# A two-layer hybrid decoder trunk on one core: where block products' weights begin in SBUF, and norms by transposes

## The chip, the cores and the metric

The kernel runs on one core of one Trainium2 chip. The metric is the device time of one execution in microseconds. All numbers are float32 in memory; most matmuls read them as float32r after a split into a first part (rounded) and a second part (what the rounding left).

## The reference

Two layers over 512 tokens of width 1024. Layer 0 mixes by sliding-window attention and a short gated convolution, layer 1 by chunked gated linear attention; behind each mixer follow a gated MLP with a causal convolution of width 3 and a gated per-layer embedding. Every part begins with an RMS norm.

```python
def _rms_norm(x, gain):
    xf = x.astype(jnp.float32)
    y = xf * lax.rsqrt(jnp.mean(xf * xf, axis=-1, keepdims=True) + RMS_EPS)
    return (y * gain.astype(jnp.float32)).astype(x.dtype)

def _conv_ffn(h, w_up, conv_w, conv_b, w_down):
    u = _causal_depthwise_conv(h @ w_up, conv_w) + conv_b
    gate, up = jnp.split(u, 2, axis=-1)
    return (jax.nn.gelu(gate, approximate=False) * up) @ w_down

def _per_layer_embedding(x, p_i, norm, w_gate, w_proj):
    gate = jax.nn.sigmoid(_rms_norm(x, norm) @ w_gate)
    return gate * (p_i @ w_proj)

def reference(x, p, ...):
    for i in range(DEPTH):
        h = _rms_norm(x, mix_norm[i])
        x = x + (_attn_conv_mixer if i % 2 == 0 else _gla_mixer)(h, ...)
        x = x + _conv_ffn(_rms_norm(x, ffn_norm[i]), ...)
        x = x + _per_layer_embedding(x, p[i], ...)
    return x
```

## The kernel before

The activations lie transposed in SBUF (`xT`, eight tiles of 128 features by 512 tokens). A weight matrix is loaded in blocks by DMAs of SyncE's queue (`raw`), and each block is split in two: ScalarE copies it into the first part `wh`, VectorE subtracts that and writes the second part `wl` (`cut`, L118 to L152). A product of the two splits takes three matmuls (`mm3`, L153): first by first, first by second, second by first.

There are two kinds of product. *Full* products (`mm3`, L157 to L159) have a stationary operand of 128 by 128 weights and stream 512 tokens. *Block products* (`seven`, L835 on, matmuls on L850 to L852) form two column blocks of the MLP's matrices by a scheme of seven products of half blocks instead of eight; each has four steps of three matmuls, and each matmul streams 256 tokens against 128 by 128 weights. Their weights are made by `first_forms`, `more_forms` and `cut_blocks` (L789 on): blocks of the matrix and differences of blocks, split into `wh` and `wl` tiles of 1024 columns or, where smaller, into tiles of 512 columns (`t2`, in the buffers of tag `sq`).

In the up-projection of each MLP (`ffn`) a loop runs over eleven groups: in each, two columns of the second half of the matrix by full products and two of the first by seven block products. The order of TensorE's instructions is written out by hand there (`manual_schedule`), and so it is in the down-projection (`down`), where a `plan` lists full and block units, and in the last stage (`ple1`), where the orders of VectorE and ScalarE are written out too. Elsewhere a planner orders the work of each engine. Each engine works its queue in order.

A norm is in three pieces. While the features of a stage come out, ScalarE squares them and VectorE adds the squares up in `acc` (128 features by 512 tokens). `end_norm` (L316) sums over features: four matmuls with `acc` as the stationary operand and one column of ones as the moving one give the sums, tokens on partitions; `rsqrt` (L161) scales them on VectorE and raises them to the power -1/2 on GpSimd, which gives `r`. Products run on unnormed activations meanwhile; their results are multiplied by the factor later. Where tokens lie along the free axis, the factor is needed on all partitions: `spread` (L329) splits `r` in two, builds two diagonal tiles `dg` on VectorE, multiplies each by a square of ones on TensorE, and ScalarE copies the result to `R`. `end_norm` takes the sums so in five norms; `spread` is called five times.

A column of vectors (biases, taps, gains) is turned by `columns` (L198), which writes it into a tile that is kept. The taps of the two MLPs have tiles of their own, `vfa0` and `vfb0`, `vfa1` and `vfb1`.

Of the kernel before, what the change touches and what calls it, by code (L numbers as in the profile page):

```python
# [14 lines left out]
ALU = mybir.AluOpType  # L15
# [41 lines left out]
class Kernel:  # L57
# [35 lines left out]
    def four(self, pool, dtype=F32R):  # L93
        return pool.tile([P, 4, S], dtype, tag="four", name=self.nm("four"), bufs=7)

    def split(self, hl, src, gain=None):

        nc = self.nc
        h, l = hl
        if gain is None:  # L100
            nc.scalar.activation(h, src, AF.Copy)
            nc.vector.tensor_tensor(l, src, h.bitcast(F32), ALU.subtract)
        else:
            nc.scalar.activation(h, src, AF.Copy, scale=gain)
# [10 lines left out]
        t = self.wp.tile([P, 2048], F32, tag="raw", name=self.nm("raw"), bufs=2)  # L115
        return t[:, : na * nb].rearrange("p (a b) -> p a b", b=nb)

    def cut(self, rv, by, pool=None, bufs=3):  # L118


        nc = self.nc
        pool = pool or self.wp
        na, nb = rv.shape[1:]
        parts = []
        n = 2 if na * nb > 1024 else 1
        for k in range(n):
            if by == "b":
                a, b = na, nb // n
                v = rv[:, :, k * b : (k + 1) * b]
            else:  # L130
                a, b = na // n, nb
                v = rv[:, k * a : (k + 1) * a, :]
            h = pool.tile([P, 1024], F32R, tag="wh", name=self.nm("wh"), bufs=bufs)
            l = pool.tile([P, 1024], F32R, tag="wl", name=self.nm("wl"), bufs=bufs)
            hv = h[:, : a * b].rearrange("p (a b) -> p a b", b=b)
            lv = l[:, : a * b].rearrange("p (a b) -> p a b", b=b)
            nc.scalar.activation(hv, v, AF.Copy)  # L137
            nc.vector.tensor_tensor(lv, v, hv.bitcast(F32), ALU.subtract)  # L138
            parts.append((hv, lv))

        def get(i, c0, c1):
            if by == "b":
                b = nb // n
                k = c0 // b
                h, l = parts[k]
                return h[:, i, c0 - k * b : c1 - k * b], l[:, i, c0 - k * b : c1 - k * b]
# [23 lines left out]
    def setup(self):  # L170
        nc, a = self.nc, self.a
        self.mhalf = self.cp.tile([P, 32], F32, name="mhalf")[:, :16]
        self.cf = self.cp.tile([P, P + 64 + 256], F32, name="cf")
        self.ident = self.cf[:, :P]
        self.ones = self.cp.tile([P, P], F32, name="ones")
        self.ones_r = self.cp.tile([P, P], F32R, name="ones_r")
        self.nowhere = self.pa()
        with self.tc.manual_schedule(engines={ET.PE, ET.DVE, ET.Activation}):
            nc.vector.memset(self.ones, 1.0)
            nc.vector.tensor_copy(self.ones_r, self.ones)  # L180
            nc.vector.memset(self.mhalf, -0.5)
            nc.scalar.dma_start(self.ident, a["cst_f"][:, :P])
            self.vec0 = self.load_vectors0()
            self.idle(7)
        self.invf = self.cf[:, P + 32 : P + 64]
        self.amask = self.cf[:, P + 64 :]

# [10 lines left out]
    def columns(self, name, views, q=None):  # L198

        nc = self.nc  # L200
        n = sum(v.shape[0] for v in views)
        rows = self.sp.tile([P, P], F32, tag="vrow", name=self.nm("vrow"))
        if q is None and self.gate is not None:
            self.late(rows[:, :1])
        at = 0
        for v in views:
            (q or nc.gpsimd).dma_start(rows[at : at + v.shape[0], :], v)
            at += v.shape[0]
        if q:

            nc.scalar.copy(self.few(4, "rs", 4), self.mhalf[:, :4])
        col = self.cp.tile([P, -(-n // 64) * 64], F32, name=name)[:, :n]
# [31 lines left out]
    def load_vectors_ffn(self, i):  # L244
        a = self.a
        w = a["ffn_conv_w"][i].rearrange("j (c p) -> j c p", p=P)
        b = a["ffn_conv_b"][i].rearrange("(c p) -> c p", p=P)
        va = self.columns(f"vfa{i}", [w[0], w[1]])
        vb = self.columns(f"vfb{i}", [w[2], b])
        self.fcv = [va[:, :44], va[:, 44:], vb[:, :44], vb[:, 44:]]  # L250


# [5 lines left out]
    def advance(self, m, gain, src=None):  # L258
# [6 lines left out]
        if m == 0:  # L265
            nc.scalar.activation(self.acc, x, AF.Square)
        else:
            sq = self.sp.tile([P, S], F32, tag="sq", name=self.nm("sq"), bufs=2)
            nc.scalar.activation(sq, x, AF.Square)
            nc.vector.tensor_tensor(self.acc, self.acc, sq, ALU.add)  # L270

    def squares(self, m):
# [1 line left out]
        if m == 0:  # L274
            nc.scalar.activation(self.acc, x, AF.Square)
        else:
            sq = self.sp.tile([P, S], F32, tag="sq", name=self.nm("sq"), bufs=2)
# [38 lines left out]
    def end_norm(self, sums=None):  # L316

        nc = self.nc
        if sums is None:
            ps = self.pa()  # L320
            for t in range(NT):
                nc.tensor.matmul(
                    ps[:, t : t + 1], self.acc[:, t * P : (t + 1) * P], self.ones[:, :1], start=True, stop=True
                )
            sums = ps[:, :NT]
        self.r = self.few(NT, "rtok")
        self.rsqrt(self.r, sums, 1.0 / D)

    def spread(self):  # L329

        nc = self.nc
        rh = self.sm.tile([P, 8], F32R, tag="rhi", name=self.nm("rhi"))[:, :NT]
        rl = self.few(NT, "rlo")
        nc.scalar.activation(rh, self.r, AF.Copy)
        nc.vector.tensor_tensor(rl, self.r, rh.bitcast(F32), ALU.subtract)
        pr = self.pa()
        for i, x in enumerate((rh.bitcast(F32), rl)):
            dg = self.sp.tile([P, NT, P], F32R, tag="sq", name=self.nm("dg"), bufs=2)
            nc.vector.tensor_tensor(
                dg, self.ident.unsqueeze(1).to_broadcast([P, NT, P]),  # L340
                x.unsqueeze(2).to_broadcast([P, NT, P]), ALU.mult,
            )
            nc.tensor.matmul(pr, self.ones_r, dg.rearrange("p a b -> p (a b)"), start=i == 0, stop=i == 1)
        R = self.sp.tile([P, S], F32, tag="R", name=self.nm("R"))
        nc.scalar.copy(R, pr)
        return R
# [77 lines left out]
    def mixer0(self):  # L424
        nc, a, tc = self.nc, self.a, self.tc
        with tc.tile_pool(name="m0", bufs=1) as mp:
# [65 lines left out]
            sink = self.sm.tile([P, 16], F32, name="sink", bufs=1)[:, :NQ]  # L492
# [182 lines left out]
            def conv_taps(j2):  # L675
                for c in range(2):
                    j = 2 * j2 + c
                    xs = mp.tile([P, S], F32, tag="cxs", name=self.nm("cxs"), bufs=2)
                    pad = mp.tile([P, S + 64], F32, tag="pad", name=self.nm("pad"), bufs=2)[:, : S + 2]
                    nc.scalar.copy(xs, pss["x", c])  # L680
                    nc.gpsimd.memset(pad[:, :2], 0.0)
                    nc.vector.tensor_tensor(pad[:, 2:], pss["c", c], R2, ALU.mult)
# [106 lines left out]
    def cut_blocks(self, src, wide=True):  # L789

        nc = self.nc
        if wide:
            h, l = (self.wp.tile([P, 1024], F32R, tag=g, name=self.nm(g), bufs=3) for g in ("wh", "wl"))
        else:
            h, l = (self.sp.tile([P, S], F32R, tag="sq", name=self.nm("t2"), bufs=2) for _ in range(2))
        h, l = (x.rearrange("p (j n) -> p j n", n=src.shape[2]) for x in (h, l))
        nc.scalar.activation(h, src, AF.Copy)  # L797
        nc.vector.tensor_tensor(l, src, h.bitcast(F32), ALU.subtract)  # L798
# [10 lines left out]
    def first_forms(self, ev, od, raw=None):  # L809
# [3 lines left out]
        if raw is not None:  # L813
            plain = self.cut_blocks(raw[:, :, :P])
        else:
            h, l = (self.wp.tile([P, 1024], F32R, tag=g, name=self.nm(g), bufs=3) for g in ("wh", "wl"))
            h, l = (x.rearrange("p (j u n) -> p j u n", u=2, n=P) for x in (h, l))
            for u, b in enumerate((b11, b21)):
                self.split((h[:, :, u], l[:, :, u]), b)
# [61 lines left out]
    def ffn(self, i, project, next_gain):  # L881
# [8 lines left out]
        with tc.tile_pool(name=f"ffn{i}", bufs=1) as fp:  # L890
# [5 lines left out]
                return fp.tile([P, 2, S], F32, tag="zt", name=self.nm("zt"), bufs=2)  # L896

            def taps(y, ps, f, more=None):
                z = fp.tile([P, S + 2], F32, tag="z", name=self.nm("z"), bufs=3)[:, :S]
                if more is None:  # L900
                    nc.vector.tensor_tensor(z, ps, R, ALU.mult)
                else:
# [398 lines left out]
    def ple1(self, fp):  # L1301
# [16 lines left out]

        def chunk(src):
            if count[0] % 6 < 3:  # L1320
                h, l = (self.wp.tile([P, 2, H], F32R, tag=g, name=self.nm(g), bufs=3) for g in ("wh", "wl"))
            else:
                four = self.four(fp)
                h, l = four[:, :2], four[:, 2:]
# [45 lines left out]
            return pj  # L1370

        def result():
            return fp.tile([P, S + 2], F32, tag="z", name=self.nm("so"), bufs=3)[:, :S]

        def keep(banks, tag):
            out = []
# [33 lines left out]
        with tc.manual_schedule(engines={ET.PE, ET.DVE, ET.Activation}):  # L1410
# [4 lines left out]
            add(None, "s1", wt1, first=True, order=steps[:2])  # L1415

            self.end_norm()
            ka = [self.sp.tile([P, S], F32, tag=g, name=self.nm("keep"), bufs=n) for g, n in (("acc", 1), ("sq", 2))]
            for k, x in zip(ka, X):
                nc.scalar.copy(k, x)  # L1420
            wt2 = chunks(b11)
# [10 lines left out]
            kb = [self.sp.tile([P, S], F32, tag="sq", name=self.nm("keep"), bufs=2), result()]  # L1432
# [45 lines left out]
    def mixer1(self):  # L1478
# [4 lines left out]
        with tc.tile_pool(name="m1", bufs=1) as mp:  # L1483
# [285 lines left out]
            def read(h):  # L1769
# [12 lines left out]
                        mm(po, Ec[:, c], st[:, j - 1, :], start=False, stop=True)  # L1782
                    pos.append(po)
                for j, po in enumerate(pos):
                    sq = self.sp.tile([P, GDV], F32, tag="sq", name=self.nm("osq"), bufs=2)
# [161 lines left out]
```

## Time and profile before

| | |
|---|---|
| median of 3 runs | 1223.96 us (1223.2 to 1224.04) |
| profiled execution, first to last instruction | 1221.9 us |
| granted TensorE clock, mean | 0.999 |
| TensorE busy | 1215.3 us, 7040 matmuls |
| VectorE busy | 972.8 us |
| ScalarE busy | 667.0 us |
| HBM | 95 GB/s over the span |

The profile page shows the busy time of each engine over the span (PE is TensorE's matmuls, PEld its weight loads, DVE VectorE, ACT ScalarE, POOL GpSimd), the span in 40 slices with the busy share in tenths, the chain of work that ended last, and the costliest groups of instructions with the names of their tiles (`pa` and `ps` are PSUM, `a`, `b` and `four` split activations). In the lists in order of time a row has the start in us, the duration in us, the engine, the line, the operation, output and inputs, and the shape. The end of a matmul is modelled, and matmuls overlap, so the time that one costs is the step from its start to the next one's start. In a table of stretches each engine has its busy time and, in brackets, the number of instructions; behind them stand the granted clock, the DMA share and GB/s.

### The profile page before, as it was taken

How to read it: one execution, taken by the hardware profiler on the slowest of the kernel's cores; microseconds unless marked ns; L12 is line 12 of the kernel's file. 1: busy time of each engine (PE TensorE's matmuls, PEld its weight loads, DVE VectorE, ACT ScalarE, POOL GpSimd, SP SyncE). 2: the span in 40 equal slices, each digit the busy share in tenths (PEclk: the TensorE clock that was granted, in tenths of full speed). 3: DMA queues.
4: the chain of work that ended last, by engine and by line, in shares of the span. 5: the costliest groups of instructions: out<-in, count | busy, mean ns of one | idle time of the engine just before them, and what ended most of it. 6: DMA issues, size and time to landing. Idle time of an engine off the chain costs nothing.

```text
span 1221.9 us, 17764 instructions
## 1 busy us (share of the span) xinstructions
PE 1215.3 (99%) x7040; PEld 1055.2 (86%) x7040; DVE 972.8 (80%) x1539; ACT 667.0 (55%) x1087; POOL 43.5 (4%) x64
## 2 busy tenths in 40 slices
PE   9999999999999999999999999999999999999998
PEld 8877789999899889888988988889999999888887
DVE  6886587899998996746679876678999888978595
ACT  7466455656555644534573555555565545645374
POOL 2500000000000000000100000000000000000000
PEclk9999999999999999999999999999999999999999
DMA  7221322423233242222322222322242423322601
GB/s 218 78 97 40 100 72 69 138 70 117 91 103 105 87 138 96 95 74 98 122 92 68 71 70 69 104 75 99 71 137 69 139 69 120 131 86 95 207 1 69
DMA packets 111271, 117.61 MB, mean 96 GB/s; under 512 B 2856, under 2 KB 106466, under 8 KB 111188
## 3 DMA queue, kind: packets, MB, share of 16 engines
q1 hardware_dynamic: 109824, 115.35, 28.9%
q8 instruction: 55, 0.90, 0.3%
q0 software_dynamic: 560, 0.42, 0.3%
q10 hardware_dynamic: 804, 0.70, 0.2%
q14 instruction: 28, 0.23, 0.1%
HBM read 114.37 MB, written 2.10 MB: 95 GB/s over the span
## 4 chain that ended last, share of the span: by engine, by line
PE 88%; DVE 8%; ACT 2%; issue 2%; POOL 1%; DVEq 0%; ACTq 0%; POOLq 0%
PE ps L157 12%; PE ps L158 12%; PE ps L159 12%; PE pa L158 7%; PE pa L157 7%; PE pa L159 7%; PE ps L850 6%; PE ps L852 6%; PE ps L851 6%; PE pa L852 2%; PE pa L851 2%; PE pa L850 2%; DVE wl L138 1%; PE ps L1347 1%; PE ps L1349 1%
## 5 line engine op out<-in xcount | busy, mean ns | idle before, releaser
L137 ACT ACTIVATE wh<-raw 128x1024 fp32r<-128x1024 f32 (+4 forms) x154 | 152.4, 992 | 150.7 <-PE ps L158 107.3
L138 DVE TENSOR_TENSOR wl<-raw,wh 128x1024 fp32r<-128x1024 f32 (+4 forms) x154 | 175.2, 1139 | 49.9 <-ACT wh L137 49.2
L797 ACT ACTIVATE wh<-raw 128x1024 fp32r<-128x1024 f32 x78 | 82.7, 1060 | 127.5 <-DVE raw L822 63.7
L910 DVE SCALAR_TENSOR_TENSOR zt<-z,vfa,zt 128x510 f32<-128x510 f32 (+1 forms) x176 | 130.8, 745 | 11.9 <-ACT zt L908 11.2
L798 DVE TENSOR_TENSOR wl<-raw,wh 128x1024 fp32r<-128x1024 f32 x78 | 95.4, 1223 | 20.3 <-ACT wh L797 20.1
L908 ACT ACTIVATE zt<-z,vfb 128x512 f32<-128x512 f32 x88 | 70.9, 808 | 23.2 <-DVE four L961 13.7
L157 PE MATMUL ps<-b,wh 128*128 128x512 f32 x192 | 76.6, 399 | 0.0
L158 PE MATMUL ps<-b,wh 128*128 128x512 f32 x192 | 75.1, 391 | 0.0
L159 PE MATMUL ps<-b,wl 128*128 128x512 f32 x192 | 75.0, 391 | 0.0
L157 PE MATMUL pa<-a,wh 128*128 128x512 f32 x176 | 69.0, 392 | 0.0
L157 PE MATMUL pa<-b,wh 128*128 128x512 f32 x176 | 69.0, 392 | 0.0
L158 PE MATMUL pa<-b,wh 128*128 128x512 f32 x176 | 69.0, 392 | 0.0
L158 PE MATMUL pa<-a,wh 128*128 128x512 f32 x176 | 69.0, 392 | 0.0
L159 PE MATMUL pa<-b,wl 128*128 128x512 f32 x176 | 68.5, 389 | 0.0
L159 PE MATMUL pa<-a,wl 128*128 128x512 f32 x176 | 68.5, 389 | 0.0
L852 PE MATMUL ps<-four,wl 128*128 128x256 f32 x232 | 65.6, 283 | 0.0
L851 PE MATMUL ps<-four,wh 128*128 128x256 f32 x232 | 65.6, 283 | 0.0
L850 PE MATMUL ps<-four,wh 128*128 128x256 f32 x232 | 65.6, 283 | 0.0
L157 PE MATMUL ps<-a,wh 128*128 128x512 f32 x160 | 63.0, 394 | 0.0
L158 PE MATMUL ps<-a,wh 128*128 128x512 f32 x160 | 62.6, 391 | 0.0
L159 PE MATMUL ps<-a,wl 128*128 128x512 f32 x160 | 62.5, 391 | 0.0
L157 PE MATMUL ps<-uh,wh 128*128 128x512 f32 x128 | 50.3, 393 | 0.0
(471 smaller groups left out, 3531.4 us busy)
## 6 DMA issues: line engine op xcount, KB each, us to landing
raw<-in_ffn_w_up_dram SPq DMA_DIRECT2D x44, 1024.0 KB, 5.0
raw<-in_ffn_w_down_dram SPq DMA_DIRECT2D x13, 1024.0 KB, 4.7
raw<-in_hy_w_in_dram SPq DMA_DIRECT2D x8, 1024.0 KB, 4.9
raw<-in_gla_w_in_dram SPq DMA_DIRECT2D x8, 1024.0 KB, 5.0
raw<-in_ffn_w_down_dram SPq DMA_DIRECT2D x8, 768.0 KB, 4.3
raw<-in_ple_w_gate_dram SPq DMA_DIRECT2D x6, 1024.0 KB, 4.7
raw<-in_hy_w_out_dram SPq DMA_DIRECT2D x16, 256.0 KB, 4.0
raw<-in_gla_w_out_dram SPq DMA_DIRECT2D x4, 1024.0 KB, 4.7
```

Source lines behind the costliest of these rows:

```text
L137: nc.scalar.activation(hv, v, AF.Copy)
L138: nc.vector.tensor_tensor(lv, v, hv.bitcast(F32), ALU.subtract)
L157: mm(out, lh, rh, start=start, stop=False, **kw)
L158: mm(out, lh, rl, start=False, stop=False, **kw)
L159: mm(out, ll, rh, start=False, stop=stop, **kw)
L797: nc.scalar.activation(h, src, AF.Copy)
L798: nc.vector.tensor_tensor(l, src, h.bitcast(F32), ALU.subtract)
L850: mm(out, wh, xh, start=first and j == 0, stop=False, **kw)
L851: mm(out, wh, xl, start=False, stop=False, **kw)
L852: mm(out, wl, xh, start=False, stop=j == ND // 2 - 1, **kw)
L908: nc.scalar.activation(y, z, AF.Identity, scale=w2[:, f : f + 1], bias=bb[:, f : f + 1])
L910: nc.vector.scalar_tensor_tensor(out=y[:, tap:], in0=z[:, : S - tap], scalar=w[:, f : f + 1], in1=y[:, tap:], op0=ALU.mult, op1=ALU.add,)
```

## The change

Three things are changed together. The tiles `wh`, `wl` and `sq` become 64 columns (256 bytes) longer, and the weights of block products begin 16 columns (64 bytes, first parts) or 48 columns (192 bytes, second parts) into them; all other uses begin at column 0 as before. In the norms the sums come from transposes of `acc` and a reduction on VectorE, and the factor is spread by transposes of `r` repeated along the free axis; the diagonal tiles, the split of `r` and the float32 tile of ones go. Other tiles shrink: the taps of the two MLPs share two buffers, `z` and `pad` lose columns that were not read, `sink` grows by 16 columns in the place of the split of `r`.

```diff
+    def wide(self, tag, at=0, dtype=F32R):
+        return self.wp.tile([P, 1024 + 64], dtype, tag=tag, name=self.nm(tag), bufs=3)[:, at : at + 1024]
+    def sq(self, dtype=F32, at=0):
+        return self.sp.tile([P, S + 64], dtype, tag="sq", name=self.nm("sq"), bufs=2)[:, at : at + S]
...
     def cut(...):
-            h = pool.tile([P, 1024], F32R, tag="wh", name=self.nm("wh"), bufs=bufs)
-            l = pool.tile([P, 1024], F32R, tag="wl", name=self.nm("wl"), bufs=bufs)
+            h, l = self.wide("wh"), self.wide("wl")
...
     def setup(self):
-        self.ones = self.cp.tile([P, P], F32, name="ones")
+        ones = self.sq()[:, :P]
...
+        self.ones = self.ones_r.bitcast(F32)
...
     def load_vectors_ffn(self, i):
-        va = self.columns(f"vfa{i}", [w[0], w[1]])
-        vb = self.columns(f"vfb{i}", [w[2], b])
+        va = self.columns("vfa", [w[0], w[1]])
+        vb = self.columns("vfb", [w[2], b])
...
     def end_norm(self, sums=None):
             for t in range(NT):
-                nc.tensor.matmul(
-                    ps[:, t : t + 1], self.acc[:, t * P : (t + 1) * P], self.ones[:, :1], start=True, stop=True
-                )
-            sums = ps[:, :NT]
+                c = slice(t * P, (t + 1) * P)
+                nc.tensor.transpose(ps[:, c], self.acc[:, c], self.ident)
+            sums = self.few(NT, "ss")
+            nc.vector.tensor_reduce(sums, ps.rearrange("p (t d) -> p t d", d=P), op=ALU.add, axis=AX.X)
...
     def spread(self):
-        rh = self.sm.tile([P, 8], F32R, tag="rhi", name=self.nm("rhi"))[:, :NT]
-        rl = self.few(NT, "rlo")
-        nc.scalar.activation(rh, self.r, AF.Copy)
-        nc.vector.tensor_tensor(rl, self.r, rh.bitcast(F32), ALU.subtract)
         pr = self.pa()
-        for i, x in enumerate((rh.bitcast(F32), rl)):
-            dg = self.sp.tile([P, NT, P], F32R, tag="sq", name=self.nm("dg"), bufs=2)
-            nc.vector.tensor_tensor(
-                dg, self.ident.unsqueeze(1).to_broadcast([P, NT, P]),
-                x.unsqueeze(2).to_broadcast([P, NT, P]), ALU.mult,
-            )
-            nc.tensor.matmul(pr, self.ones_r, dg.rearrange("p a b -> p (a b)"), start=i == 0, stop=i == 1)
+        for t in range(NT):
+            c = slice(t * P, (t + 1) * P)
+            nc.tensor.transpose(pr[:, c], self.r[:, t : t + 1].to_broadcast([P, P]), self.ident)
...
     def cut_blocks(self, src, wide=True):
         if wide:
-            h, l = (self.wp.tile([P, 1024], F32R, tag=g, name=self.nm(g), bufs=3) for g in ("wh", "wl"))
+            h, l = self.wide("wh", 16), self.wide("wl", 48)
         else:
-            h, l = (self.sp.tile([P, S], F32R, tag="sq", name=self.nm("t2"), bufs=2) for _ in range(2))
+            h, l = (self.sq(F32R, at) for at in (16, 48))
...
     def first_forms(self, ev, od, raw=None):
-            h, l = (self.wp.tile([P, 1024], F32R, tag=g, name=self.nm(g), bufs=3) for g in ("wh", "wl"))
+            h, l = self.wide("wh", 16), self.wide("wl", 48)
...
     conv_taps, ffn, ple1:
-                    pad = mp.tile([P, S + 64], F32, tag="pad", name=self.nm("pad"), bufs=2)[:, : S + 2]
+                    pad = mp.tile([P, S + 2], F32, tag="pad", name=self.nm("pad"), bufs=2)
-                z = fp.tile([P, S + 2], F32, tag="z", name=self.nm("z"), bufs=3)[:, :S]
+                z = fp.tile([P, S], F32, tag="z", name=self.nm("z"), bufs=3)
```

The other places that made tiles of tags `wh`, `wl` and `sq` call `wide` and `sq` with no offset.

More of the change, by code (lines that the diff above doesn't have):

```diff
@@ L116, in raw, with cut @@
         return t[:, : na * nb].rearrange("p (a b) -> p a b", b=nb)
-    def cut(self, rv, by, pool=None, bufs=3):
+    def cut(self, rv, by):
         nc = self.nc
-        pool = pool or self.wp
         na, nb = rv.shape[1:]
@@ L178, in setup @@
         with self.tc.manual_schedule(engines={ET.PE, ET.DVE, ET.Activation}):
-            nc.vector.memset(self.ones, 1.0)
-            nc.vector.tensor_copy(self.ones_r, self.ones)
+            nc.vector.memset(ones, 1.0)
+            nc.vector.tensor_copy(self.ones_r, ones)
             nc.vector.memset(self.mhalf, -0.5)
@@ L211, in columns @@
             nc.scalar.copy(self.few(4, "rs", 4), self.mhalf[:, :4])
-        col = self.cp.tile([P, -(-n // 64) * 64], F32, name=name)[:, :n]
+        col = self.cp.tile([P, -(-n // 64) * 64], F32, tag=name, name=self.nm(name), bufs=1)[:, :n]
         def finish():
@@ L267, in advance @@
         else:
-            sq = self.sp.tile([P, S], F32, tag="sq", name=self.nm("sq"), bufs=2)
+            sq = self.sq()
             nc.scalar.activation(sq, x, AF.Square)
@@ L276, in squares @@
         else:
-            sq = self.sp.tile([P, S], F32, tag="sq", name=self.nm("sq"), bufs=2)
+            sq = self.sq()
             nc.scalar.activation(sq, x, AF.Square)
@@ L491, in mixer0 @@
                 C, Sn = self.rope_tables(mp)
-            sink = self.sm.tile([P, 16], F32, name="sink", bufs=1)[:, :NQ]
+            sink = self.sm.tile([P, 32], F32, name="sink", bufs=1)[:, :NQ]
             self.late(sink[:, :1])
@@ L1320, in chunk @@
             if count[0] % 6 < 3:
-                h, l = (self.wp.tile([P, 2, H], F32R, tag=g, name=self.nm(g), bufs=3) for g in ("wh", "wl"))
+                h, l = (self.wide(g).rearrange("p (a b) -> p a b", b=H) for g in ("wh", "wl"))
             else:
@@ L1372, in result @@
         def result():
-            return fp.tile([P, S + 2], F32, tag="z", name=self.nm("so"), bufs=3)[:, :S]
+            return fp.tile([P, S], F32, tag="z", name=self.nm("so"), bufs=3)
         def keep(banks, tag):
@@ L1417, in ple1 @@
             self.end_norm()
-            ka = [self.sp.tile([P, S], F32, tag=g, name=self.nm("keep"), bufs=n) for g, n in (("acc", 1), ("sq", 2))]
+            ka = [self.sp.tile([P, S], F32, tag="acc", name=self.nm("keep"), bufs=1), self.sq()]
             for k, x in zip(ka, X):
@@ L1431, in ple1 @@
             add(None, "s2", wt2, order=steps[4:])
-            kb = [self.sp.tile([P, S], F32, tag="sq", name=self.nm("keep"), bufs=2), result()]
+            kb = [self.sq(), result()]
             for k, x in zip(kb, X):
@@ L1784, in read @@
                 for j, po in enumerate(pos):
-                    sq = self.sp.tile([P, GDV], F32, tag="sq", name=self.nm("osq"), bufs=2)
+                    sq = self.sq()[:, :GDV]
                     nc.scalar.activation(sq, po, AF.Square, accum_out=oss[:, j : j + 1])
```

## The prediction

> **What bounds the kernel now.** The page comes first: who is busy, when, and what the chain of waits is made of.
>
> ```profile
> span 1221.9 us, 17764 instructions
> PE 1215.3 (99%) x7040; PEld 1055.2 (86%) x7040; DVE 972.8 (80%) x1539; ACT 667.0 (55%) x1087; POOL 43.5 (4%) x64
> DVE  6886587899998996746679876678999888978595
> PE 88%; DVE 8%; ACT 2%; issue 2%; POOL 1%; DVEq 0%; ACTq 0%; POOLq 0%
> ```
>
> TensorE hardly ever waits: 88% of the chain that ends last is PE. So time is gained or lost by the rate at which matmuls follow one another, not by waits. The busy time cannot show that rate, since the end of a matmul is modelled and runs into the next one. The start times can, so next I read TensorE's instructions in order of time, where a run of full products (L157 to L159, 512 moving columns) passes into a run of block products (L850 to L852, 256 columns) and back.
>
> ```profile
> 230.24 0.39 PE L157 MATMUL pa<-a,wh 128*128 128x512 f32 x1
> ...
> 230.92 0.28 PE L850 MATMUL pa<-a,wh 128*128 128x256 f32 x1
> 231.03 0.28 PE L851 MATMUL pa<-a,wh 128*128 128x256 f32 x1
> 231.15 0.28 PE L852 MATMUL pa<-a,wl 128*128 128x256 f32 x1
> 231.27 0.28 PE L850 MATMUL pa<-a,wh 128*128 128x256 f32 x1
> ...
> 232.23 0.28 PE L852 MATMUL pa<-a,wl 128*128 128x256 f32 x1
> 232.35 0.40 PE L157 MATMUL pa<-a,wh 128*128 128x512 f32 x1
> 232.59 0.40 PE L158 MATMUL pa<-a,wh 128*128 128x512 f32 x1
> ```
>
> From 230.24 to 230.92 three full products start: 227 ns each. From 231.27 to 232.23 eight block products start: 120 ns each. The 256 columns between the two shapes cost 107 ns, so 256 columns alone stream in 107 ns, and each matmul of either shape pays 13 ns more than it streams. That surcharge is what a change in the weights' start can touch. It is not fixed: the first block product after full ones takes 0.11 us (230.92 to 231.03), and the first full one after block products 0.24 us (232.35 to 232.59), with the same shapes. How many block products there are, by line, over the whole span:
>
> ```profile
> 0.00:1222.00 1222.00, 229.93 (x812) 155.36 (x812) 1.00 0.30 96
> 0.00:1222.00 1222.00, 229.73 (x812) 155.38 (x812) 1.00 0.30 96
> 0.00:1222.00 1222.00, 229.79 (x812) 155.39 (x812) 1.00 0.30 96
> ```
>
> The count stands in brackets: 812 on each of L850, L851 and L852, so 2436, about 292 us at 120 ns. The eighth of a microsecond is paid often enough that 1 ns on it is 2.4 us of the kernel.
>
> **The change, part by part.** *Block weights.* By the tile sizes in the code every operand of the split products begins a 256-byte line now, except the odd rows of the value weights (below). The change moves only the stationary operand of block products: first parts to byte 64, second parts to byte 192. No row of this trace has a stationary operand there, so the price must be bounded. The nearest rows are the value projection of the second mixer, where the moving operand of 336 columns (1344 bytes a row) begins 64 bytes past a line in every second row:
>
> ```profile
> 664.08 0.32 PE L157 MATMUL ps<-wh,b 128*128 128x336 f32 x1
> 664.24 0.31 PE L158 MATMUL ps<-wl,b 128*128 128x336 f32 x1
> 664.39 0.32 PE L159 MATMUL ps<-wh,b 128*128 128x336 f32 x1
> 664.54 0.32 PE L157 MATMUL ps<-wh,b 128*128 128x336 f32 x1
> ...
> 665.00 0.32 PE L157 MATMUL ps<-wh,b 128*128 128x336 f32 x1
> ```
>
> Six starts in 0.92 us are 153 ns; 336 columns stream in 140 ns (336 times 107/256), so the surcharge is 13 ns there as well, though single steps differ (0.16, 0.15, 0.15). A shifted moving operand thus changes the pattern and not the mean. That argues for little effect, but the shape is not the same: in a block product the load of the next 128 weight columns runs beside all of a 107 ns stream, in these beside part of a longer one.
>
> Bounds: below, the surcharge vanishes and a block product takes its 107 ns of streaming, 2436 times 13.3 ns = 32 us gained. Above, it grows to that of the 0.24 us step, 0.24 - 0.213 = 27 ns at two decimals, another 13 ns, 32 us lost. Between them I take 113 ns, the middle between 107 and 120 and also the step that this very shape shows once in each run (0.11 us): 2436 times 6.7 ns = 16.2 us gained. That the surcharge varies at fixed addresses says that it comes from how the weight load and the moving stream meet in time, so that a new start should alter it; the direction is not in the rows. The Trainium skill gives a least step of its own ("TensorE: Matmul & The Clock Gate", section "Wait — 56ns, not 53.3ns?"): a warm matmul costs its columns at 2.4 GHz plus a fixed 2.5 ns, which would be 109 ns for 256 columns and 26 us for the lot; the rows above pay 13 ns, so here the measurement disagrees as long as the operands stand as they do.
>
> Is the gain kept? VectorE makes the second parts of these weights, and in the up-projection it is nearly full. Three stretches of the length of one group (21 us), columns PE, PEld, DVE, ACT, POOL:
>
> ```profile
> 282.00:303.00 21.00, 21.00 (x133) 19.06 (x132) 20.91 (x30) 13.73 (x21) 0.00 (x0) 1.00 0.29 94
> 345.00:366.00 21.00, 21.00 (x134) 19.04 (x133) 18.75 (x25) 11.39 (x16) 0.00 (x0) 1.00 0.30 102
> 902.00:923.00 21.00, 21.00 (x133) 19.07 (x132) 20.37 (x29) 13.36 (x21) 0.00 (x0) 1.00 0.32 101
> ```
>
> A group has seven products of twelve matmuls, 84, and would become 0.56 us shorter. Late groups (18.75 us of VectorE) have 2.25 us to spare; the few early ones of each layer have 0.09 to 0.63 us. I give back 1 us for these. With it the weights bring -15.2 us. The copies that write the shifted tiles keep their element counts; I cost their new starts at nothing, and whatever they cost is hidden behind the same slack.
>
> *Norms.* The sums now come from four transposes and a reduction on VectorE instead of eight passes against the ones; the spread takes four transposes instead of two products, two diagonal tiles and a split.
>
> ```profile
> 599.71 0.95 PE L322 MATMUL pa<-ones,acc 128*128 128x1 f32 x8
> 600.52 0.41 PE L157 MATMUL ps<-wh,b 128*128 128x368 f32 x1
> ...
> 202.45 0.61 PE L343 MATMUL pa<-dg,ones_r 128*128 128x512 f32 x2
> 202.90 0.28 PE L850 MATMUL ps<-four,wh 128*128 128x256 f32 x1
> ...
> 546.16 1.03 PE L1253 MATMUL pa<-cf,pin 128*128 128x128 f32 x8
> 546.95 0.48 PE L157 MATMUL ps<-a,wh 128*128 128x512 f32 x1
> 547.26 0.40 PE L158 MATMUL ps<-a,wh 128*128 128x512 f32 x1
> ```
>
> Eight passes hold TensorE 0.81 us; eight transposes 0.79 us, so four 0.40: -0.41 us, in five norms. Two spread products hold it 0.45 us; four transposes 0.40 and 0.08 for the slower full product behind them (0.31 against 0.227): +0.03, five times +0.15 in all. TensorE goes straight on in four of these norms, so there the gain is real: 4 times -0.41 = -1.64. In the fifth, in the last stage, VectorE sets the end, and the reduction joins its queue:
>
> ```profile
> 45.03 0.69 DVE L503 TENSOR_REDUCE ss<-m 128x8 f32<-128x512 f32 x1 [2.47 <-ACT m L501]
> 1171.42 0.15 DVE L166 TENSOR_SCALAR rs<-pa 128x4 f32<-128x4 f32 x1
> ```
>
> ```profile
> 1175.05 2.27 DVE raw L1336 x2
> 1177.32 1.19 DVE wl L1327
> 1179.59 1.23 DVE wl L1327
> 1180.86 0.50 PE pa L158
> ```
>
> The only reduction of 512 elements takes 0.69 us. Here it stands ahead of L166, behind which the weight differences (L1336) and second parts (L1327) are queued, and the projection (PE L158) waits for the last of them: +0.69 us, and TensorE's 0.41 is lost in that wait. Elsewhere the factor comes 0.7 us later, before the spread; but the spread then no longer needs the split and two diagonal tiles,
>
> ```profile
> 199.99 0.69 DVE L339 TENSOR_TENSOR dg<-cf,rhi 128x512 fp32r<-128x512 f32 x1
> ```
>
> at 0.69 us each, so the spread is ready earlier than before. Norms in all: -1.64 + 0.15 + 0.69 = -0.8 us; between -1.9 (the reduction hidden) and +0.8 (only the last norm felt).
>
> *The rest.* The second layer's convolution columns now share a buffer with the first's; their load stands in the second mixer, after the first layer's last read of them, so no new wait. The ones share memory with the warm-up's tile: the same three instructions. Other tiles keep lines that begin at 0; only the shifted inputs of the short convolution and its results move, and VectorE and ScalarE alone read them. No DMA is added or moved. All of this I cost at nothing.
>
> **Sum.** 1221.9 us of the profiled execution - 15.2 - 0.8 = 1205.9; the runs' median of 1223.96 stands 2.1 us above that span: 1208.0 us.
>
> **The rivals.** *Nothing happens to the matmuls:* the 336-column rows keep their 13 ns with a shifted moving operand, which speaks for it; the differing steps at one address speak against it. Then only the norms remain: 1223.2 us. A rule of the Trainium skill would have it so ("SBUF — State Buffer", section "Door 1: The DMA port swizzle", the note on cachelines): lines are 16 bytes, so a weight row of 512 bytes fills 32 of them from byte 0, 64 or 192 alike. No run here shows the line's size.
>
> *The shift costs:* a weight row of 512 bytes fills two 256-byte lines now, and three from byte 64 or 192. If the 13.3 ns are paid by line, 6.7 each, a block product takes 127 ns: 2436 times 6.7 = +16.2, and VectorE then has more room, so nothing comes off: 1223.96 + 16.2 - 0.8 = 1239.4 us. It decides as soon as the step passes 120.3 ns (0.8 us over 2436). For it speaks that the surcharge is the same at every width, like a fixed number of lines per load; against it, that the steps of one shape range from 0.11 up without a change in lines.
>
> *VectorE becomes the bound:* steps of 107 ns would shorten a group by 1.1 us, more than the early groups have. If half of what the lower bound brings in four early groups of each layer (8 times 84 times 13.3 ns = 8.9 us, so 4.5) is lost: 1223.96 - 32 + 4.5 - 0.8 = 1195.7 us.
>
> **How the numbers follow.** Forecast (a gain, at 109 to 119 ns): 0.50; VectorE as the bound: 0.08; nothing: 0.12; the shift costs: 0.30. What a measurement tells from no change is 0.2%, 2.4 us: a step between 119.3 and 121.3 ns. Faster 0.58, same 0.12, slower 0.30. The forecast's own range is 1199 to 1221. Since the costly case has 0.30, the whole range reaches into it: 1198 to 1237, which leaves out its upper part (0.12) and the strongest gain (0.06).
>
> **What would show it.** In TensorE's order of time: block products starting every 113 ns (120 and no gain, 127 and a loss), full products still every 227. The groups of the up-projection: 20.4 us instead of 21.0. The first norm: transposes at 0.40 us in place of L322. In the last stage: the second part at 1179.59 later against the stage's start by 0.7 us. Wrong it would be if block products keep their step and the time still moves, if waits of TensorE on second parts appear beyond 1 us, or if the full products change pace.

## The result, and the profile after

| | before | after |
|---|---|---|
| median | 1223.6 us (4 runs, 1223.2 to 1224.04) | 1211.6 us (4 runs, 1210.77 to 1213.89) |
| profiled execution, first to last instruction | 1221.9 us | 1209.4 us |
| VectorE busy | 972.8 us | 967.9 us |

The ratio is 0.9905 with a 95% interval of 0.9891 to 0.9919: 12.0 us less in the medians, 12.5 us in the profiled executions. The forecast was 1208.0 us, with 1199 to 1221 as its own range.

The page of the changed kernel: span, busy times, VectorE's slices, and the chain that ended last by engine.

```profile
span 1209.4 us, 17733 instructions
PE 1201.5 (99%) x7030; PEld 1039.7 (86%) x7030; DVE 967.9 (80%) x1529; ACT 664.9 (55%) x1082; POOL 44.5 (4%) x64
DVE  6786587899898996746679876687999999978595
PE 88%; DVE 7%; ACT 2%; issue 1%; POOL 1%; DVEq 0%; ACTq 0%; POOLq 0%
```

TensorE is as full as it was, and its share of the chain is the same 88%. The time came from the rate at which its instructions follow one another. TensorE's instructions in order of time (start, duration, engine, line, tiles, shape) at the place that the prediction read before:

```profile
228.83 0.39 PE L163 MATMUL pa<-a,wh 128*128 128x512 f32 x1
229.06 0.39 PE L164 MATMUL pa<-a,wl 128*128 128x512 f32 x1
229.28 0.28 PE L848 MATMUL pa<-a,wh 128*128 128x256 f32 x1
229.40 0.28 PE L849 MATMUL pa<-a,wh 128*128 128x256 f32 x1
...
229.87 0.28 PE L850 MATMUL pa<-a,wl 128*128 128x256 f32 x1
...
233.43 0.28 PE L848 MATMUL ps<-a,wh 128*128 128x256 f32 x1
...
235.92 0.28 PE L849 MATMUL ps<-four,sq 128*128 128x256 f32 x1
```

The last two rows are 22 steps apart: 2.49 us, 113 ns each. But the first five steps behind the full product (229.28 to 229.87) take 118 ns on the mean. The full products still take 227 ns. A group of the up-projection, where nothing waits, takes 20.59 us from one group's first block product to the next one's, 21.04 before.

The starts are what can be trusted in these rows, so I added up the steps from each TensorE instruction's start to the next one's, by the kind of the earlier instruction, over both traces:

```
kind of instruction            before us (count)   after us (count)   difference
block products                 292.21 (2436)       280.24 (2436)      -11.97
full products, 512 columns     784.20 (3401)       783.91 (3391)       -0.29
passes against the ones          4.14 (40)           0                 -4.14
transposes, 128 columns         23.45 (204)         27.19 (244)        +3.74
all others                                                              about 0
```

The 3401 contain the ten products of the spread, whose steps come to 2.38 us in the trace of before, and the fifteen of the warm-up, which took 0.42 us less; without both, full products lost 2.5 us. Most of that is steps that contain a wait. Here is TensorE's one new long wait, in the last stage, with VectorE's queue ahead of it:

```profile
1166.87 0.50 PE L162 MATMUL pa<-wh,four 128*128 128x512 f32 x1
1168.31 0.51 PE L163 MATMUL pa<-wl,four 128*128 128x512 f32 x1 [0.95 <-DVE wl L1325]
```

```profile
1158.15 0.69 DVE L331 TENSOR_REDUCE ss<-pa 128x4 f32<-128x512 f32 x1
1158.87 0.17 DVE L171 TENSOR_SCALAR rs<-ss 128x4 f32<-128x4 f32 x1
...
1164.76 2.36 DVE L1325 TENSOR_TENSOR wl<-raw,wh 128x1024 fp32r<-128x1024 f32 x2
1167.04 1.22 DVE L1325 TENSOR_TENSOR wl<-four,wh 128x1024 fp32r<-128x1024 f32 x1
```

The step from 1166.87 to 1168.31 is 0.93 us longer than the same step before, and the one ahead of it 0.19 us longer. About another 1 us lies at the change from full to block products in some groups of the up- and down-projections, as here:

```profile
941.10 0.39 PE L164 MATMUL pa<-b,wl 128*128 128x512 f32 x1
941.71 0.39 PE L848 MATMUL ps<-four,wh 128*128 128x256 f32 x1 [0.22 <-ACT ps L869]
```

### The profile page after: what moved, and what is told of

Read it like the earlier page. It is cut to its first block, busy times and chain, and to the rows that moved or that the text cites. A ratio compares the mean times of both kernels' runs of the same rounds, so it can differ in the third digit from the quotient of the medians.

```text
span 1209.4 us, 17733 instructions
## 1 busy us (share of the span) xinstructions
PE 1201.5 (99%) x7030; PEld 1039.7 (86%) x7030; DVE 967.9 (80%) x1529; ACT 664.9 (55%) x1082; POOL 44.5 (4%) x64
## 4 chain that ended last, share of the span: by engine, by line
PE 88%; DVE 7%; ACT 2%; issue 1%; POOL 1%; DVEq 0%; ACTq 0%; POOLq 0%
PE ps L162 12%; PE ps L163 12%; PE ps L164 12%; PE pa L163 7%; PE pa L162 7%; PE pa L164 7%; PE ps L848 6%; PE ps L850 5%; PE ps L849 5%; PE pa L848 2%; PE pa L850 2%; PE pa L849 2%; DVE wl L143 1%; PE ps L1345 1%; PE ps L1347 1%
```

## The experiments

Each is an edit of the changed kernel; a time is the median of 4 or 10 runs, for the kernels under "Other starts" of one run. "Block sum" is the first row of the table above.

**Norms alone, and starts alone.**

The first has all block weights at byte 0 (here and where `sq` is called); the second has the old `end_norm` and `spread`, as the minus lines of the change show them, and the new starts.

```diff
-            h, l = self.wide("wh", 16), self.wide("wl", 48)
+            h, l = self.wide("wh", 0), self.wide("wl", 0)
```

> The changed kernel with all weights at byte 0 again: only the norms and the tile sizes differ from the kernel before. If the block weights' start brought the gain (my theory), block products start every 120 ns again and the time is 1222 to 1224 us, 0.4 to 0.8 us under the kernel before. If the norms brought it (rival), it stays near 1211.6 us.

> The changed kernel with the old sums (eight passes against the ones) and the old spread (split, two diagonal tiles, two products); block weights at bytes 64 and 192. My theory: block products every 113 to 115 ns, and 1211 to 1213 us, since the norms are worth less than 1 us and cost the last stage a wait; that wait of TensorE on a second part (0.9 us in the last stage) should be gone. Rival (norms): near 1223 us.

Norms alone: 1222.08 us, ratio 0.9991 (0.9982 to 1.0), span 1220.3; that is 1.3 us under the kernel before, where 0.4 to 0.8 was expected. Its block sum is 292.37 us, and the steps are those of before again (16 of them here, 120 ns each):

```profile
234.05 0.28 PE L848 MATMUL pa<-four,wh 128*128 128x256 f32 x1
...
235.97 0.28 PE L849 MATMUL ps<-four,sq 128*128 128x256 f32 x1
```

Starts alone: 1215.4 us, ratio 0.9941 (0.9924 to 0.9957), block sum 281.25. So the pace belongs to the start of the weights and to nothing else in the change. But against the 1223.35 us that the kernel before took beside them, 8.0 and 1.3 us make 9.3, not 12.0, and the second kernel missed what was expected of it by 2 to 4 us; that is taken up below.

**The same start for full products.**

```diff
     def cut(...):
-            h, l = self.wide("wh"), self.wide("wl")
+            h, l = self.wide("wh", 16), self.wide("wl", 48)
```

> The changed kernel with the weights of full products at bytes 64 and 192 as well. If the surcharge of 13.3 ns is one and the same thing in both shapes (theory of the meeting of weight load and stream, taken alone), full products fall from 227 to about 220 ns: some 3000 of them, about 20 us less, 1191 us. Rival: in a full product the weight load covers only half of the stream and the surcharge stays or grows: 227 to 233 ns, 1211 to 1230 us.

1220.42 us, ratio 0.9978 (0.9969 to 0.9987). The block sum stays low (280.47), but the full products take 794.46 us, 10.6 more than in the changed kernel: the rival's time, and no surcharge that is one and the same thing in both shapes. Three full products in a row now start 233 ns apart, where they started 227 apart:

```profile
229.06 0.39 PE L164 MATMUL pa<-a,wl 128*128 128x512 f32 x1
...
229.76 0.40 PE L164 MATMUL pa<-a,wl 128*128 128x512 f32 x1
```

Over the trace the three of them take some 231, 229 and 236 ns. What is good for a stream of 256 columns is bad for one of 512.

This kernel shows one thing more. In some products the weights are not the stationary operand but the moving one (in the lists the moving operand stands first, so `wh,a` streams the weights), and `cut` makes these weights too. The 96 products of 256 columns at the program's start are such; first the changed kernel, 12 steps of 120 ns, then this one, 15 steps of 118:

```profile
16.94 0.28 PE L162 MATMUL pa<-wh,a 128*128 128x256 f32 x1
...
18.38 0.28 PE L162 MATMUL pa<-wh,a 128*128 128x256 f32 x1
```

```profile
16.14 0.28 PE L162 MATMUL pa<-wh,a 128*128 128x256 f32 x1
...
17.91 0.28 PE L162 MATMUL pa<-wh,a 128*128 128x256 f32 x1
```

The 96 products of 512 columns that stream weights (`ps<-wh,a`) went from 227 to 230 ns. So the start of the moving operand counts too, with the same sign in each shape as that of the stationary one.

**Other starts.** Five kernels in which only the bytes differ at which first and second parts begin.

```diff
-            h, l = self.wide("wh", 16), self.wide("wl", 48)
-            h, l = (self.sq(F32R, at) for at in (16, 48))
+            h, l = self.wide("wh", A), self.wide("wl", B)
+            h, l = (self.sq(F32R, at) for at in (A, B))
```

> Both parts of block weights at byte 64. If only the number of 256-byte lines that a weight row touches counts (three instead of two), this is the same as 64 and 192: 113 to 115 ns, 1211 to 1212 us. If the relative start counts, the step of block products differs from 113 by some ns, up to 120 (1224 us).

> Both parts of the block products' weights begin 192 bytes into 256-byte lines (first parts before: 64; everything else as in the changed kernel). Both parts at byte 64 gave a mean step of 117.5 ns between block products, 64 and 192 in turn 113 to 115. Theory 'own start': each start has a step of its own, and 192 is the better one; then the pure rows of 192 step at 109 to 111 ns, the block products fall to 265 to 272 us in sum, and the run is 1203 to 1208 us. Rival 'taking turns': what counts is that a row and the next begin at different offsets; then 117 ns, block sum 286 to 288 us, and 1215 to 1218 us, as with both at byte 64.

> Both parts at byte 128, half a 256-byte line. Theory 'own start, smooth': between the steps for byte 64 (117.5 ns) and byte 192. Theory 'taking turns': 117 ns again and 1215 to 1218 us. Rival '128-byte lines': 128 is as good as 0, so 120 ns, block sum 291 to 293 us, 1220 to 1223 us.

> First parts of the block products' weights at byte 64, second parts at byte 0 of the 256-byte lines. So far, as mean steps between block products: 0/0 120, 64/64 117.5, 192/192 118, 128/128 120.4, 64/192 113 to 115. Theory A: what helps is that the two parts begin 128 bytes apart; then this pair, 64 apart, has no such gain and lies between its own parts, 118.5 to 120 ns, block sum 288 to 292 us, 1217 to 1222 us. Theory B: any difference helps; then 115 ns or less, block sum below 284 us, 1211 to 1214 us.

> First parts at byte 0, second parts at byte 128. Theory A (128 bytes apart helps, by the 4 to 5 ns that 64/192 lies below 64/64 and 192/192): about 115.5 ns, block sum 279 to 283 us, 1211 to 1214 us. Theory B (any difference helps) says the same. Theory C: the pair must be away from the bounds of 128 bytes as well, by itself no gain comes from the distance; then 120 ns as 0/0 and 128/128 have it, block sum 291 to 294 us, 1220 to 1224 us.

```
bytes (first/second)   block sum us   a step in the middle of a run, ns   time us
0/0 (norms only)       292.37         120.0                               1222.08
128/128                293.54         119.9                               1223.4
0/128                  290.97         119.4                               1221.48
64/0                   288.13         117.9                               1218.16
64/64                  287.35         117.6                               1216.89
192/192                287.06         117.4                               1215.38
64/192 (the change)    280.24         113.4                               1211.6
```

The step is the mean over each trace, from the eighth block product of a run to its last but one and without steps above 150 ns, which contain a wait. It shows in these rows, of 192/192 (15 steps) and of 128/128 (16 steps):

```profile
233.63 0.28 PE L848 MATMUL ps<-a,wh 128*128 128x256 f32 x1
...
235.39 0.28 PE L848 MATMUL ps<-four,sq 128*128 128x256 f32 x1
```

```profile
233.98 0.28 PE L848 MATMUL ps<-a,wh 128*128 128x256 f32 x1
...
235.90 0.29 PE L849 MATMUL ps<-four,sq 128*128 128x256 f32 x1
```

A weight row that begins 64 or 192 bytes into a line touches three 256-byte lines instead of two, and is faster: the rival that charged by lines is gone. An own step for each start doesn't carry the whole either: 64 and 192 are equal alone (117.6 and 117.4) and 4 ns better together. Nor is it enough that the parts are 128 bytes apart (0/128: 119.4) or that they differ (64/0: 117.9). So 64/0 took the time that theory A gave it, but 0/128, for which A had 115.5 ns, took that of theory C, and A falls with B; that 128 is like 0 bears out the rival of 128-byte lines as far as 128/128 goes, and no further. Times of single runs that lie within 2 us of each other are not told apart; the steps are steadier, 113.4 or 113.5 ns in each of the six kernels of this document that have 64/192 for block weights and byte 0 for full ones. Of what was tried, gains above 1 ns come only with a part at byte 64 or 192, and the largest when the two parts take different ones of these. Why is open: no row shows what the load and the stream do inside a step.

**The last stage.** The sums of its norm by the old passes, all else as changed.

```diff
     def ple1(...):
-            self.end_norm()
+            self.end_norm(ones=True)
```

> The changed kernel, but the sums of the norm in the last stage are formed by the old matmuls against ones, so that no reduction stands in VectorE's queue ahead of the second parts of the last stage's weights. Theory (the last part of my sum): TensorE's wait of 0.95 us on these second parts goes, the four sums cost TensorE some 0.4 us more, and the time falls by 0.4 to 0.9 us, to 1210.7 to 1211.2 us where the changed kernel has 1211.6. Rival: the wait is only moved to the next second part or to the final additions, and the time is within 0.2 us of the changed kernel's.

1211.62 us, ratio 0.9903 (0.9888 to 0.9918): the same as the changed kernel, so the rival's time, but not by its mechanism. The wait is gone; TensorE takes the second part 0.52 us behind the first again:

```profile
1169.02 0.39 PE L162 MATMUL pa<-wh,four 128*128 128x512 f32 x1
1169.54 0.50 PE L163 MATMUL pa<-wl,four 128*128 128x512 f32 x1
```

I laid the same instructions of the two traces side by side. Before the last stage this kernel is 1.9 us behind the changed one, from waits in the up-projections, although up to the last stage every engine has the same instructions in the same order in both programs. In the last stage it loses 0.4 us by the passes and gains 1.1 by the wait, 0.7 net. So the term is confirmed inside the trace, and in the medians it drowns: runs of one kernel here differ by 2 to 3 us (1210.48 to 1212.4 for this one). And since the two programs are alike up to the last stage, the 1.9 us suggest that stalls of this size come and go from one execution to the next.

**What belongs to neither part alone.** The starts with the new spread but the old sums:

> The weights' starts and the new spread by transposes, with all norms' sums by the old matmuls against ones. Starts alone gave 1215.4 us, everything together 1211.6, the norms alone 1.3 us less than before: about 2.5 us of the whole belong to neither part alone. Theory: the stalls in the second feed-forward layer's up-projection of the starts-only kernel (TensorE waiting six times for ScalarE's copy, which stands in its queue behind an activation that VectorE feeds late) go once VectorE no longer forms the spread's diagonal tiles, so this kernel lacks them: 1211 to 1213 us. Rival: the stalls hang on the phase into which the groups happen to fall, or on the sums: then they are still there, and it takes 1214 to 1216 us.

1216.14 us, ratio 0.994 (0.9924 to 0.9957). My theory, that the diagonal tiles on VectorE made the stalls, falls: they are gone here and the stalls are not. What is missing of the change are the sums alone. Five sums cost TensorE some 2.2 us more by the old way, less 0.9 for the wait they avoid; in the medians some 3 us remain. In the profiled execution, the slowest of the four (1218.25 us), stalls in the second layer's up-projection come to more than that, as the last table here shows. TensorE waits there for a copy on ScalarE (L869, L873) that stands behind work which itself waits, for VectorE and for the weights' transfer. ScalarE's order of time in this kernel:

```profile
1007.96 1.06 ACT L1037 ACTIVATE zt<-zt 128x1024 f32<-128x1024 f32 x1 [1.08 <-DVE zt L908]
1008.93 0.36 ACT L869 COPY ps<-ps 128x256 f32<-128x256 f32 x1
...
1012.77 1.06 ACT L142 ACTIVATE wh<-raw 128x1024 fp32r<-128x1024 f32 x1 [1.64 <-DMA raw<-in_ffn_w_up_dram]
1013.74 0.37 ACT L873 COPY ps<-ps 128x256 f32<-128x256 f32 x1
```

So I split the activation on L1037 in two, on the changed kernel and on this one, to let the copy between:

```diff
-                    nc.scalar.activation(g, g, AF.Gelu)
+                    [nc.scalar.activation(g[:, u], g[:, u], AF.Gelu) for u in range(2)]
```

> The changed kernel with the GELU of a group's pair of blocks as two activations of 512 columns instead of one of 1024, by which ScalarE's copy for the block products (line 869) comes to stand between the halves, or ahead of work that waits for VectorE's last tap. Theory: the stalls at the change from full to block products, some 2.8 us in sum in the changed kernel, come from this copy standing behind the GELU; they fall by 0.5 to 1.5 us and the kernel takes 1210.0 to 1211.2 us. Rival: VectorE and the weights' transfers set when all of this is ready, so the stalls only change place: 1211.0 to 1213 us.

> The same edit on the kernel with the starts and the new spread but the old sums, which took 1216.1 us with about 5 us more of stalls in the second feed-forward layer's up-projection than the changed kernel. Theory (the copy behind the GELU): these stalls fall by more than 2 us, to 1212 to 1214 us. Rival (the ring of weight transfer, split and release is late, the copy also stands behind splits that wait for transfers): 1215 to 1217 us.

1213.27 us, ratio 0.9915 (0.9901 to 0.993), and 1219.94 us, ratio 0.9968 (0.9959 to 0.9978): neither is faster. The first cannot be told from the changed kernel (0.9891 to 0.9919), the second is slower than the kernel it was made from, and by more than the rival had. Two halves take 2 times 634 ns of ScalarE where one took 1062, and TensorE now waits for the copies of the next product (L859). This theory falls too. ScalarE's waits for the up-projection's transfers (line waited on, us in total, times, longest), from 815 to 1045 us, of the changed kernel and of the last one:

```profile
ACT wh L795 <- DMA raw<-in_ffn_w_up_dram: 4.1, 3, 1.6
```

```profile
ACT wh L795 <- DMA raw<-in_ffn_w_up_dram: 16.9, 7, 3.4
ACT wh L142 <- DMA raw<-in_ffn_w_up_dram: 2.4, 5, 0.6
```

```
kernel                    ScalarE's wait for these     how far TensorE falls behind the
                          transfers, 815 to 1045, us   changed kernel, 829 to 1055, us
changed                    4.1                          0
last sums by ones         11.3                          1.1
starts only               13.7                          3.0
starts and spread         15.5                          5.7
GELU halves               16.2                          2.3
spread, GELU halves       19.3                          8.2
```

Each row is one execution, so differences of 2 us say nothing here. Of these kernels, those that fall behind are those whose splits wait long for transfers, though not in strict order. The wait alone doesn't make the stall: the kernel before has 6.1 us of it and the one with the new start for full products 10.6, and in neither does TensorE wait for such a copy in this stretch. A transfer starts when VectorE has read the buffer for the last time, and VectorE is full just ahead of the stalls. Two stretches of the changed kernel, one group long each (columns as in the prediction, VectorE third):

```profile
882.00:903.00 21.00, 21.00 (x136) 18.96 (x135) 20.95 (x30) 13.36 (x22) 0.00 (x0) 1.00 0.29 92
923.00:944.00 21.00, 20.78 (x132) 18.31 (x131) 19.03 (x25) 11.98 (x18) 0.00 (x0) 1.00 0.35 115
```

VectorE has 0.05 us to spare in the first, and in the second TensorE has lost 0.22. That fits a ring of split, release, transfer and split that runs as fast as TensorE does now and carries a delay from group to group. That it is this ring was argued from the waits and not tried. Open is also why the old sums set it off and the new ones don't.

## Why the prediction was right, and where it was off

**The bound, and what the surcharge is.** Right: the pace and no wait made the time. With the weights at byte 0 the pace of before came back, and with it all but 1.3 us of the time. That a new start would alter the surcharge was right too, but that it comes from how weight load and stream meet in time is not shown. One reading fell: that a shifted moving operand leaves the mean as it is. It held for the rows of 336 columns, and with the weights of full products shifted, streams of 256 columns became 2 ns faster and those of 512 columns 3 ns slower.

**The step of 113 ns.** Right in the middle of a run: 113.4 ns, 6.6 less than 120, 2436 times 6.6 = 16.1 us against 16.2 forecast. That the number came out so was luck: it was the middle between two bounds, the direction was not in the rows, and the same working would have given 113 to any pair of starts, where the five others that were tried take 117.4 to 119.9. The step that failed is a smaller one: the forecast applied it to all block products alike. There are 116 runs of 12 to 36 block products, all but a few behind full products. Medians of their first five steps were 113, 119, 120, 120, 120 ns before and are 119, 117, 122, 116, 114 now: 588 against 592, 4 ns gained where 33 were forecast. 29 ns times 116 runs are 3.4 us. With 0.5 us of waits inside the runs, 16.1 - 3.4 - 0.5 = 12.2, measured 11.97. A group of the up-projection shows the same: it has four such runs and became 0.45 us shorter, not 0.56. The row of 0.11 us that I took as a sign of what the shape can do became one of the slow steps, 119 ns.

**What VectorE gives back.** Forecast 1 us, found about 1.4 us of waits, if all of them are put down to VectorE, which was not shown: 0.9 us at the changes from full to block products beyond those of before, 0.5 within the runs. The size was nearly right, the condition was not: I counted the early groups' 0.09 to 0.63 us of slack as a loss once. The kernels of the last table show that this loss can grow to 3 or 8 us by changes that hardly touch the amount of work, which nothing in the working foresaw.

**The norms.** Forecast -0.8, measured -1.6 in the span of the kernel with norms alone and -1.3 in its median. The four transposes of a sum hold TensorE 0.36 us, where 0.40 was forecast; the matmul behind them takes 0.08 more than its like, as it did behind the old passes:

```profile
201.42 0.60 PE L341 MATMUL pa<-cf,rtok 128*128 128x128 f32 x4
201.77 0.36 PE L848 MATMUL ps<-four,wh 128*128 128x256 f32 x1
...
592.70 0.60 PE L329 MATMUL pa<-cf,acc 128*128 128x128 f32 x4
593.06 0.41 PE L162 MATMUL ps<-wh,b 128*128 128x368 f32 x1
593.31 0.33 PE L163 MATMUL ps<-wl,b 128*128 128x368 f32 x1
```

Over both traces, 40 passes (4.14 us) and ten spread products (2.38) gave way to 40 transposes (3.74): -2.8 us. Behind four of the spreads the next matmul takes 0.08 more than before, which leaves -2.4, where the working had 5 times -0.41 + 0.15 = -1.9. The transposes of a spread were forecast at 0.40 us as eight of another place took 0.79, and they take 0.35 (201.42 to 201.77). The last stage cost 1.1 of this (0.93 and 0.19); the forecast, 0.69 and TensorE's 0.41 lost, said 1.1. The reduction is 0.69 us long and stands where it was said to stand.

**The sum.** -12.0 (block products, two of the matmuls behind spreads among them), -2.6 + 1.1 (the rest of the norms), +0.9 (changes between kinds): -12.6; the spans differ by 12.5, the rest being small terms of both signs.

**The rivals.** "Nothing" falls by the norms-only kernel: 120 ns come back. Of the Trainium skill's note ("SBUF — State Buffer", section "Door 1: The DMA port swizzle"), by which lines are 16 bytes, so that bytes 0, 64 and 192 would be alike, the runs say this: the starts aren't alike for TensorE's reads, 120 against 113 ns; what the size of a line is, no run shows. "The shift costs" has its price on the other shape: full products at the same starts take 10.6 us more, but the same three lines a row go with a loss there and a gain here, so their count explains neither. "VectorE becomes the bound" came in part, in single groups, long before steps of 107 ns. The step by the rule of the Trainium skill ("TensorE: Matmul & The Clock Gate", section "Wait — 56ns, not 53.3ns?"), an estimate of 109 ns for 256 columns, isn't reached by any of the seven pairs of starts; the best stays 4 ns above it.

**The median.** The span came out 2.2 us below the runs' median, as 2.1 us was forecast. Of that, 1.8 us is what a run's time has over its own span (1211.17 against 1209.4); the rest depends on which run was profiled.

## What to carry to other kernels

Where TensorE never waits, read the step from start to start for each shape, subtract what the columns alone take, and try where the weights begin, for each shape by itself: the same start brought one shape 12 us and cost another 10. Multiply a gain per step by the steps that lie in the middle of a run only, and look at the first few behind another shape. When TensorE gets faster, waits that were hidden come out, here some 1.4 us in the changed kernel and more in others, and the two parts' gains measured alone (8.0 and 1.3 us) did not add up to the whole (12.0).

## What the hardware showed beside

The pace of back-to-back matmuls with unchanged shapes and data depends on where the rows of an operand begin. With stationary weights it was 120 ns at byte 0 and 113 at bytes 64 and 192 for 256 columns, and for 512 columns 227 at byte 0 and 229 to 236 at bytes 64 and 192, the order reversed. With weights as the moving operand the same starts gave 120 against 118 ns for 256 columns and 227 against 230 for 512. And behind full products whose weights begin at byte 0 the faster pace needs about five matmuls to settle (119, 117, 122, 116, 114, then 113 ns); where the full products' weights begin at bytes 64 and 192 too, it needs two (119, 119, then 114). None of the runs tells why.
